# One hybrid attention block on one core: five forms of the last factor kept on chip, plain blocks written beside the second group, decays placed in the first pair

## The chip, the core and the metric

The kernel runs on one core of a Trainium2 chip. The engines of the core are TensorE (PE, matrix products), VectorE (DVE, elementwise work and scans), ScalarE (ACT, activations and casts), GpSimd (POOL) and SyncE (SP), which issues most of the transfers. Each engine executes its own instructions in order; between engines there are semaphores. The metric is the device time of one execution in microseconds, lower is better.

## The reference, cut to what matters

One layer on 512 tokens of width 2048, in fp32: a normalisation, one wide input projection, two groups of heads, gates, one output projection with the residual.

```python
h = rms_norm(x, norm_gain)
proj = einsum('bsd,de->bse', h, w_in)          # 14 groups of 512 columns and a rest of 16
(sb_q, sb_k, sb_v, sb_g, gl_q, gl_k, gl_v, gl_g, gl_lr) = split(proj)
a_out = stick_breaking_attention(rms_norm(q), rms_norm(k), v)     # 8 heads x 128
a_out = rms_norm(a_out) * silu(sb_g)
log_alpha = log_sigmoid(gl_lr @ gla_w_alpha + gla_b_alpha) / 16
b_out = gated_linear_attention(gl_q, gl_k, gl_v, log_alpha)       # 4 heads, key 128, value 256
b_out = rms_norm(b_out) * silu(gl_g)
x = x + concat([a_out, b_out]) @ w_out          # 4 groups of 512 columns
```

The cumulated log_alpha of a chunk gives the decay factors exp(cum) and exp(-cum), by which queries and keys of the second group are multiplied.

## The kernel before, in words

**Numbers.** A product in fp32 is made of three products of fp32r parts: every operand is split into hi (a cast, on ACT) and lo (the difference, on DVE). Weights are loaded from memory in tiles of 128 x 1024 (512 KB) by `load` (L162, tile names st_ and pw_) into three buffers st and four buffers pw, and `split` (L169 the cast, L170 the difference) fills one of three hi and three lo buffers.

**Groups.** The 14 + 4 groups of 512 weight columns go in this order: q and k (`direct`, eight steps each, one per weight tile), then eight pairs by `pair`: qv, vk, gqk, gv, ga, gb with the factor h, then o0 and o1 with the factor m. A pair is a product of 2 x 2 blocks with seven block products instead of eight. It has four parts: products A11 with D, then NQ with S4 (weight tiles b), then A12 with S3 (tiles c and d), then A22 (e, from pw). Tile names carry the pair and the part: hi_qvd2 is the hi part of tile d of unit 2 in pair qv. Units u are 0 to 3, in o0 and o1 in the order 0, 1, 3, 2. y and x are the two accumulators of a pair.

**Forms of the factor.** The factor of a pair is used in seven forms per unit: the plain blocks A11, A12, A22 and the sums D, NQ, S4, S3, each split into hi and lo (L279 to L283; 512 KB for both). The class `Acts` holds them. Forms named in its list `keep` stay on chip in slots of the ring u4 (25 slots of 512 KB, counted by `held`; `ut` takes one, `drop` gives some back, `room` asks). All other forms are put in one of four buffers of the pool as, written to memory once (`_write`, L255, far_ names) and read again by each later pair (L245). For h, `block` makes the plain blocks during q and writes them there; they stay in the ring until k is done. For both h and m the list is D and S3. The sums are made on DVE (L201 to L227).

**Work beside the products.** Attention, decays, gated linear attention and gates are generators ("side chains") that emit a few instructions each time a product calls `side.step()`. A chain that yields a number waits for that many microseconds of the planner's own clock `side.t`, which adds up a modelled duration of every matmul; one that yields a condition waits until that holds. The order of PE is the order in which the program emits its instructions. The orders of DVE, ACT, POOL and SP are made by a scheduler that prefers instructions emitted inside `urgent()`.

**Chains the change touches.** `decays` (L679 on) waits for the low-rank product, then 50 planner microseconds, then for five free slots; for each of four heads it makes one small matmul lg, on ACT lgs, three functions lge, the small amid and the factors qe, ke (L695 to L710), and on DVE L700, the scan L702, L707, gm L713, L715 and L716. It is spawned between the pairs qv and vk. `gate` (four of them, two halves each) multiplies a gate by its head outputs (ge, L980), waits 12 or 8 planner microseconds, transposes the result on PE (mT, L115) and fills the factor m (me, mo). `attention` makes scores zA, zB, zC, their cumulated sums cs_A, cs_B, cs_C (DVE L867 and L868), weights (ACT L873) and transposes them (wT_A, wT_B, wT_C).

`used` and `ready` are called by a pair at the start of its parts (0: A11, 2: NQ and S4, 3: A12 and S3) and give back slots; after q, k, qv, gb and o0 further slots are given back.

Of the kernel before, what the change touches and what calls it, by code (L numbers as in the profile page):

```python
# [15 lines left out]
D = 2048  # L16
# [77 lines left out]
def body(ctx: ExitStack, tc: tile.TileContext, x, xT, w_in, w_lr, w_alpha, vecs, w_out, out):  # L94
# [87 lines left out]
    class Acts:  # L182
# [74 lines left out]
        def block(self, odd, half, u, last):  # L257

            f = f"A{half + 1}{odd + 1}"
            if (f, u) not in self.near:  # L260
                name = f"{f}_{self.tag}{u}"
                with urgent():
                    if f == "A21":
                        t = wpool.tile([P, 2, KU, H2], F32R, name=name, tag="pw", bufs=HU)
                    else:
                        t = ut(name, F32R).rearrange("p h (k t) -> p h k t", k=KU)
                    self._split(t, f, u)
                    if f != "A21":
                        self._write(t, f, u, name)
                self.near[f, u] = t  # L270
            if last and f != "A21":
                drop(1)
            return self.near[f, u]
# [40 lines left out]
    def pair(A, s1, s2, tag, o1, o2, order=(0, 1, 2, 3), tmajor=True, before=None):  # L314
# [91 lines left out]
        o1.finish(y, 0, 1.0, m1)  # L406
        for u in order:
            w = split(pw[u], f"{tag}e{u}")
            mult("A22", u, w, x, False, u == last)
# [269 lines left out]
    def decays():  # L679
        yield lambda: "lr" in done  # L680
        yield 50.0
        yield room(5)
# [7 lines left out]
        for h in range(GH):  # L690
# [29 lines left out]
            if h < GH - 1:  # L720
                yield 8.0
        done.add("decays")
# [240 lines left out]
    def gate(gi):  # L963
# [3 lines left out]
        def chain(half, z):  # L967
# [13 lines left out]
            drop(1)  # L981
            yield 12.0 if gi < 2 else 8.0
            yield lambda: gi in me or held[0] + 2 <= NU4
# [33 lines left out]
    def used(stage, u):  # L1017
        if stage == 3 and u == 0:
            drop(6)

    direct(h, w_in[0], "q", normed("q0", qn[0]), before=first_loads)
    side.spawn(x_norm())
    direct(h, w_in[2], "k", normed("k0", kn[0]), extra=rank_products, last=True)
    side.spawn(low_rank())
    side.until(lambda: "rstd" in done)
    v[0] = ByToken("sv0", by_rstd)
    pair(h, w_in[1], w_in[4], "qv", normed("q1", qn[1]), v[0], before=used)
    drop(4)
    side.spawn(attention(0, qn[0], kn[0], v[0]))
    side.spawn(decays())  # L1030
    v[1] = ByToken("sv1", by_rstd)
# [9 lines left out]
    pair(h, w_in[6], w_in[7], "ga", gate(0), gate(1))  # L1041
    m = Acts("m", lambda u: me[u], lambda u: mo[u], ("D", "S3"))

# [4 lines left out]
    def ready(stage, u):  # L1048
        if stage == 0:
            side.until(lambda: m_done[u] == 2)  # L1050

    order = (0, 1, 3, 2)
    pair(m, w_out[0], w_out[1], "o0", Residual(0), Residual(1), order=order, before=ready)
    drop(10)
    pair(m, w_out[2], w_out[3], "o1", Residual(2), Residual(3), order=order)
# [44 lines left out]
```

## Time and profile before

| what | us |
|---|---|
| median of the runs | 901.11 (898.07 to 902.56, three runs) |
| the profiled execution | 900.33 |
| its span | 898.6 |
| PE busy | 823.4 (92%) |
| DVE busy | 627.7 (70%) |
| ACT busy | 517.3 (58%) |
| transfers | 216.99 MB, mean 241 GB/s |

The span runs from the first instruction to the last of the profiled execution; the granted clock of TensorE was 0.982 of full speed in the mean. q ends at about 61 us, k at 115, qv at 200, vk and gqk at 429, gv at 520, ga at 625, gb at 714, o0 at 814, o1 at 894. In a list of waits each row is an engine, what it waited to do, the releaser, the microseconds in total, how often, and the longest. A busy share is a mean over stages; what counts for a stage is which wait ends last in it.

### The profile page before, as it was taken

How to read it: one execution, taken by the hardware profiler on the slowest of the kernel's cores; microseconds unless marked ns; L12 is line 12 of the kernel's file. 1: busy time of each engine (PE TensorE's matmuls, PEld its weight loads, DVE VectorE, ACT ScalarE, POOL GpSimd, SP SyncE). 2: the span in 40 equal slices, each digit the busy share in tenths (PEclk: the TensorE clock that was granted, in tenths of full speed). 3: DMA queues.
4: the chain of work that ended last, by engine and by line, in shares of the span. 5: the costliest groups of instructions: out<-in, count | busy, mean ns of one | idle time of the engine just before them, and what ended most of it. 6: DMA issues, size and time to landing. Idle time of an engine off the chain costs nothing.

```text
span 898.6 us, 11580 instructions
## 1 busy us (share of the span) xinstructions
PE 823.4 (92%) x4082; PEld 684.2 (76%) x4082; DVE 627.7 (70%) x760; ACT 517.3 (58%) x947; POOL 68.5 (8%) x113
## 2 busy tenths in 40 slices
PE   7899989989998599989999899999998888889997
PEld 5688878778787499989787687877886766667875
DVE  4542858578777886788754685467956899786754
ACT  5465587358867598656563446556644745443322
POOL 1000000100132100210200010010001000000000
PEclk9999999999999799999999999999999999999999
DMA  8878327995497453787448971798579635999895
GB/s 311 299 288 297 138 81 246 295 367 193 164 282 213 143 207 125 253 225 263 162 163 266 335 270 64 247 290 307 197 252 303 236 140 207 313 347 394 283 328 164
DMA packets 62042, 216.99 MB, mean 241 GB/s; under 512 B 7040, under 2 KB 7168, under 8 KB 61984
## 3 DMA queue, kind: packets, MB, share of 16 engines
q1 hardware_dynamic: 54928, 195.26, 60.0%
q0 software_dynamic: 4608, 16.78, 10.3%
q10 hardware_dynamic: 2448, 4.21, 1.2%
q8 instruction: 32, 0.52, 0.2%
q14 instruction: 26, 0.21, 0.1%
HBM read 191.06 MB, written 25.17 MB: 241 GB/s over the span
## 4 chain that ended last, share of the span: by engine, by line
PE 21%; DMA 14%; DVE 9%; issue 3%; ACT 3%; DVEq 0%; SPq 0%; ACTq 0%
PE x_o L111 5%; PE y_o L111 4%; DMA st_gvd<-in_w_in 2%; PE y_gb L111 2%; PE x_gb L111 2%; PE x_ga L111 2%; DMA st_gad<-in_w_in 2%; DMA st_gbd<-in_w_in 2%; PE y_ga L111 1%; DMA st_o0d<-in_w_out 1%; DMA st_o1c<-in_w_out 1%; PE x_gv L111 1%; DMA pw_gb<-in_w_in 1%; DMA A_h<-far_A_h 1%; DMA A_m<-far_A_m 1%
## 5 line engine op out<-in xcount | busy, mean ns | idle before, releaser
L111 PE MATMUL z_q<-hi_q,A_h 128*128 128x512 f32 x128 | 33.3, 411 | 8.3 <-DVE A_h L283 3.3
L111 PEld LDWEIGHTS z_q<-hi_q,A_h 128*128 128x128 f32 x128 | 24.9, 197 | 16.4 <-DVE A_h L283 4.2
L111 PE MATMUL z_k<-hi_k,A_h 128*128 128x512 f32 x128 | 30.6, 391 | 0.0
L111 PEld LDWEIGHTS z_k<-hi_k,A_h 128*128 128x128 f32 x128 | 23.5, 188 | 4.8 <-ACT n_q L147 0.2
L170 DVE TENSOR_TENSOR lo_k<-st_k,hi_k 128x1024 fp32r<-128x1024 f32 x8 | 9.8, 1223 | 24.1 <-ACT hi_k L169 13.8
L180 POOL DMA_DIRECT2D pw_o<-in_w_out x8 | 7.0, 871 | 179.2 <-DVE S_m L283 79.5
L180 POOL DMA_DIRECT2D pw_qv<-in_w_in x4 | 3.6, 907 | 174.0 <-DVE st_qvd L175 174.0
L873 ACT ACTIVATE cs_B<-cs_B 128x512 f32<-128x512 f32 x8 | 5.1, 632 | 19.4 <-POOL cs_B L871 18.0
L111 PE MATMUL z_q<-lo_q,A_h 128*128 128x512 f32 x64 | 15.8, 389 | 0.0
L111 PE MATMUL z_k<-lo_k,A_h 128*128 128x512 f32 x64 | 15.8, 389 | 0.0
L115 PE MATMUL wT_B<-ident,cs_B 128*128 128x128 f32 x32 | 5.4, 294 | 11.0 <-DVE cs_A L868 10.4
L111 PE MATMUL x_o<-hi_o0d,S_m 128*128 128x512 f32 x32 | 10.0, 451 | 5.7 <-ACT hi_o0d L169 2.4
L115 PE MATMUL mT<-ident,ge 128*128 128x128 f32 x64 | 8.7, 280 | 6.0 <-DVE ge L980 6.0
L973 ACT ACTIVATE ge<-z 128x1024 f32<-128x1024 f32 x8 | 8.5, 1058 | 9.7 <-DVE z L969 9.7
L170 DVE TENSOR_TENSOR lo_q<-st_q,hi_q 128x1024 fp32r<-128x1024 f32 x8 | 9.7, 1225 | 6.2 <-ACT A_h L282 3.3
L111 PEld LDWEIGHTS z_q<-lo_q,A_h 128*128 128x128 f32 x64 | 12.0, 188 | 2.5
L111 PEld LDWEIGHTS z_k<-lo_k,A_h 128*128 128x128 f32 x64 | 12.0, 188 | 2.5
L175 DVE TENSOR_TENSOR st_gvd<-pw_gv,st_gvd 128x1024 f32<-128x1024 f32 x4 | 4.9, 1226 | 12.6 <-DMA st_gvd<-in_w_in 12.4
L595 ACT ACTIVATE xt<-xt 128x1024 f32<-128x1024 f32 x8 | 8.5, 1058 | 8.6 <-DMA xt<-in_x 8.5
L115 PEld LDWEIGHTS wT_B<-ident,cs_B 128*128 128x128 f32 x32 | 4.0, 150 | 12.3 <-DVE cs_A L868 10.8
L115 PEld LDWEIGHTS mT<-ident,ge 128*128 128x128 f32 x64 | 7.4, 142 | 7.8 <-issue 5.7
L111 PEld LDWEIGHTS x_o<-hi_o0d,S_m 128*128 128x128 f32 x32 | 6.4, 208 | 8.8 <-ACT hi_o0d L169 2.8
(630 smaller groups left out, 2645.8 us busy)
## 6 DMA issues: line engine op xcount, KB each, us to landing
A_h<-far_A_h SPq DMA_DIRECT2D x72, 512.0 KB, 6.1
NQ_h<-far_NQ_h SPq DMA_DIRECT2D x20, 512.0 KB, 4.3
S_h<-far_S_h SPq DMA_DIRECT2D x20, 512.0 KB, 4.2
far_A_h<-A_h SPq DMA_DIRECT2D x12, 512.0 KB, 4.5
far_A_m<-A_m SPq DMA_DIRECT2D x12, 512.0 KB, 7.3
A_m<-far_A_m SPq DMA_DIRECT2D x12, 512.0 KB, 8.0
st_q<-in_w_in SPq DMA_DIRECT2D x8, 512.0 KB, 5.4
st_k<-in_w_in SPq DMA_DIRECT2D x8, 512.0 KB, 4.9
```

The source lines that it names most:

```text
L111: nc.tensor.matmul(o, l, r, **kw)
L115: nc.tensor.transpose(o, i, ident)
L170: nc.vector.tensor_tensor(lo, t, hi.bitcast(F32), ALU.subtract)
L175: (eng or nc.vector).tensor_tensor(o, a, b, op)
L180: nc.gpsimd.dma_start(t, src, accum_op=ALU.add)
L595: nc.scalar.activation(xt, xt, AF.Square, accum_out=ss8[:, j * 2 + i:j * 2 + i + 1])
L873: nc.scalar.activation(cs, cs, AF.Exp)
L973: nc.scalar.activation(e, z, AF.Exp, scale=-1.0)
```

## The change

Four things are changed.

1. `block` no longer writes the plain blocks of h when they are made in q; the write is emitted at the block's last use, in k.
2. `decays` is spawned before pair qv and waits 4 planner microseconds instead of 50, and 10 instead of 8 between heads. Slots are given back accordingly: ten at part 3 of qv.
3. The wait of a gate before its transpositions is 12 planner microseconds for all but one half of gate 2, where it is 8; before it was 12 for gates 0 and 1 and 8 for gates 2 and 3.
4. For m the list `keep` becomes D, S4, S3, A12, A22: only A11 and NQ are written and read again. Slots for the three are found by giving back slots of me and mo during o0: `pair` calls `before` at part 4 too.

```diff
@@ block
                     self._split(t, f, u)
-                    if f != "A21":
-                        self._write(t, f, u, name)
                 self.near[f, u] = t
             if last and f != "A21":
+                with urgent():
+                    self._write(self.near[f, u], f, u, f"{f}_{self.tag}{u}")
                 drop(1)
@@ pair, last part
         for u in order:
+            if before is not None:
+                before(4, u)
             w = split(pw[u], f"{tag}e{u}")
@@ decays
         yield lambda: "lr" in done
-        yield 50.0
+        yield 4.0
...
             if h < GH - 1:
-                yield 8.0
+                yield 10.0
@@ gate
-            yield 12.0 if gi < 2 else 8.0
+            yield 8.0 if gi == 2 and half == 1 else 12.0
@@ the sequence of the program
         if stage == 3 and u == 0:
-            drop(6)
+            drop(10)
...
     side.spawn(low_rank())
+    side.spawn(decays())
...
     pair(h, w_in[1], w_in[4], "qv", normed("q1", qn[1]), v[0], before=used)
-    drop(4)
     side.spawn(attention(0, qn[0], kn[0], v[0]))
-    side.spawn(decays())
...
-    m = Acts("m", lambda u: me[u], lambda u: mo[u], ("D", "S3"))
+    m = Acts("m", lambda u: me[u], lambda u: mo[u], ("D", "S4", "S3", "A12", "A22"))
...
         if stage == 0:
             side.until(lambda: m_done[u] == 2)
+        elif stage == 3 and u == order[0]:
+            drop(2)
+        elif stage == 4 and u == order[0]:
+            drop(4)
...
-    drop(10)
+    drop(4)
     pair(m, w_out[2], w_out[3], "o1", Residual(2), Residual(3), order=order)
```

In the built program SP issues 24 transfers fewer; DVE, ACT and PE have the same instructions in another order. Three places show it. A row is the line, the operation, what it writes and from what, and the shape.

SP in the q stage, before (st_q are weight tiles, he and ho parts of the input, far_ the copies in memory of the plain blocks of h):

```order
L533 DMA ho0_154<-in_xT 128x1024
L255 DMA far_A11_h0_125<-A11_h0_122 128x1024
L162 DMA st_q01_202<-in_w_in 128x1024
L162 DMA st_q11_262<-in_w_in 128x1024
L255 DMA far_A12_h0_167<-A12_h0_164 128x1024
L255 DMA far_A22_h0_172<-A22_h0_169 128x1024
L533 DMA he1_198<-in_xT 128x1024
L162 DMA st_q02_306<-in_w_in 128x1024
L162 DMA st_q12_348<-in_w_in 128x1024
L533 DMA ho1_240<-in_xT 128x1024
```

and now:

```order
L535 DMA ho0_152<-in_xT 128x1024
L162 DMA st_q01_196<-in_w_in 128x1024
L162 DMA st_q11_254<-in_w_in 128x1024
L162 DMA st_q02_294<-in_w_in 128x1024
L535 DMA he1_192<-in_xT 128x1024
L162 DMA st_q12_334<-in_w_in 128x1024
L162 DMA st_q03_374<-in_w_in 128x1024
L535 DMA ho1_232<-in_xT 128x1024
L255 DMA far_A11_h0_500<-A11_h0_122 128x1024
L162 DMA st_q13_414<-in_w_in 128x1024
L255 DMA far_A22_h0_555<-A22_h0_165 128x1024
L255 DMA far_A12_h0_553<-A12_h0_162 128x1024
L255 DMA far_A11_h1_637<-A11_h1_202 128x1024
```

The writes of A11, A12, A22 of unit 0 and A11 of unit 1 have moved behind ho1; the rows of SP that follow stand nearly as they did, with the other writes among them.

DVE at the end of pair vk, before (lgs, lge, gm, qe, ke belong to the decays; vke and gqka to the products; e_A and cs_A to the attention):

```order
L700 SCALAR_TENSOR_TENSOR lgs1_2500<-lgs1_2500,lge1_2502 128x512
L861 SCALAR_TENSOR_TENSOR e_A011_2611<-zA011_2606,e_A011_2611 128x512
L170 TENSOR_TENSOR lo_vke3_2764<-pw_vk3_1848,hi_vke3_2763 128x1024
L175 TENSOR_TENSOR pw_gqk2_2953<-pw_gqk2_2953,st_gqka2_2951 128x1024
L702 SCALAR_TENSOR_TENSOR lge1_2502<-blk_2408,lgs1_2500 128x512
L867 SCALAR_TENSOR_TENSOR cs_A011_2617<-runs_86,e_A011_2611 128x512
L707 TENSOR_TENSOR lgs1_2500<-lge1_2502 128x512
L868 TENSOR_TENSOR cs_A011_2617<-zA011_2606,cs_A011_2617 128x512
L713 TENSOR_TENSOR gm1_2513<-qe0_2411,amid1_2508 128x3
L715 SCALAR_TENSOR_TENSOR qe0_2411<-qe0_2411,rbc_105 128x512
L716 TENSOR_TENSOR ke0_2412<-ke0_2412,rbc_105 128x512
```

DVE in the second half of pair qv, now:

```order
L702 SCALAR_TENSOR_TENSOR lgs0_1415<-lgs0_1415,lge0_1417 128x512
L175 TENSOR_TENSOR st_qvd2_1490<-pw_qv2_1068,st_qvd2_1490 128x1024
L170 TENSOR_TENSOR lo_qvc2_1493<-st_qvc2_1488,hi_qvc2_1492 128x1024
L704 SCALAR_TENSOR_TENSOR lge0_1417<-blk_1406,lgs0_1415 128x512
L170 TENSOR_TENSOR lo_qvd2_1498<-st_qvd2_1490,hi_qvd2_1497 128x1024
L709 TENSOR_TENSOR lgs0_1415<-lge0_1417 128x512
L170 TENSOR_TENSOR lo_qvc3_1552<-st_qvc3_1547,hi_qvc3_1551 128x1024
L715 TENSOR_TENSOR gm0_1428<-qe0_1409,amid0_1423 128x3
L718 TENSOR_TENSOR ke0_1410<-ke0_1410,rbc_105 128x512
L175 TENSOR_TENSOR st_qvd3_1549<-pw_qv3_1107,st_qvd3_1549 128x1024
L717 SCALAR_TENSOR_TENSOR qe0_1409<-qe0_1409,rbc_105 128x512
L170 TENSOR_TENSOR lo_qvd3_1557<-st_qvd3_1549,hi_qvd3_1556 128x1024
```

The pieces of the decays, which stood among the last tiles of vk and ahead of cs_A, now stand among the tiles c and d of qv.

SP in pair o0, in the part with A12 and S3, before (A_m names are plain blocks of m, xr parts of the residual input):

```order
L162 DMA st_o0c1_6867<-in_w_out 128x1024
L255 DMA far_S4_m2_6776<-S4_m2_6770 128x1024
L255 DMA far_NQ_m2_6801<-NQ_m2_6798 128x1024
L255 DMA far_A12_m0_6836<-A12_m0_6833 128x1024
L162 DMA st_o0d1_6869<-in_w_out 128x1024
L162 DMA st_o0c3_6915<-in_w_out 128x1024
L255 DMA far_A12_m1_6884<-A12_m1_6881 128x1024
L162 DMA st_o0d3_6917<-in_w_out 128x1024
L255 DMA far_A12_m3_6932<-A12_m3_6929 128x1024
L162 DMA st_o0c2_6963<-in_w_out 128x1024
L162 DMA st_o0d2_6965<-in_w_out 128x1024
```

and now:

```order
L245 DMA A11_m0_7099<-far_A11_m0_6374 128x1024
L162 DMA st_o0c1_6857<-in_w_out 128x1024
L255 DMA far_NQ_m2_6793<-NQ_m2_6790 128x1024
L162 DMA st_o0d1_6859<-in_w_out 128x1024
L245 DMA A11_m1_7122<-far_A11_m1_6414 128x1024
L162 DMA st_o0c3_6903<-in_w_out 128x1024
L245 DMA A11_m3_7161<-far_A11_m3_6483 128x1024
L245 DMA A11_m2_7200<-far_A11_m2_6543 128x1024
L162 DMA st_o0d3_6905<-in_w_out 128x1024
L162 DMA st_o0c2_6949<-in_w_out 128x1024
L162 DMA st_o0d2_6951<-in_w_out 128x1024
```

The writes of S4, A12 and A22 are gone; reads of A11, which stood behind them for pair o1, have moved up between the loads c and d.

## Rows read from the trace of the kernel before

**Rows 1.** Windows: start:end, length, busy PE, PEld, DVE, ACT, POOL; clock, DMA share, GB/s.
```profile
200.00:270.00 70.00, 67.61 (x342) 55.87 (x340) 53.59 (x62) 55.92 (x123) 11.54 (x23) 1.00 0.65 218
714.00:771.00 57.00, 48.94 (x208) 36.59 (x207) 56.67 (x72) 32.62 (x45) 0.86 (x1) 1.00 0.56 189
771.00:794.00 23.00, 17.47 (x73) 13.02 (x71) 16.40 (x20) 9.79 (x14) 2.09 (x3) 1.00 1.00 309
794.00:814.00 20.00, 18.38 (x73) 14.81 (x74) 17.56 (x21) 8.04 (x9) 0.53 (x1) 0.91 1.04 379
814.00:894.00 80.00, 76.50 (x334) 62.34 (x334) 49.29 (x48) 26.12 (x25) 3.48 (x4) 1.00 0.88 296
```

**Rows 2.** Waits of PE over the span: us in total, times, longest.
```profile
PE wT_B L115 <- DVE cs_A L868: 10.4, 1, 10.4
PE mT L115 <- DVE ge L980: 6.0, 3, 3.6
PE x_qv L111 <- ACT hi_qvd L169: 4.0, 2, 3.1
PE x_o L111 <- ACT hi_o1d L169: 3.3, 2, 2.0
...
PE x_o L111 <- ACT hi_o0d L169: 2.4, 1, 2.4
...
PE x_o L111 <- DMA A_m<-far_A_m: 1.4, 1, 1.4
```

**Rows 3.** Timeline of PE: start, us, instructions, idle before and its releaser.
```profile
20.56 0.51 PE L111 MATMUL z_q<-hi_q,A_h 128*128 128x512 f32 x1 [1.59 <-ACT A_h L282]
...
38.45 0.49 PE L111 MATMUL z_q<-hi_q,A_h 128*128 128x512 f32 x1 [1.35 <-ACT A_h L282]
...
293.79 1.07 PE L111 MATMUL x_vk<-lo_vke,A_h 128*128 128x512 f32 x4
305.26 1.12 PE L115 MATMUL wT_B<-ident,cs_B 128*128 128x128 f32 x4 [10.40 <-DVE cs_A L868]
...
688.44 1.40 PE L115 MATMUL mT<-ident,ge 128*128 128x128 f32 x8 [3.62 <-DVE ge L980]
```

**Rows 4.** Groups of DVE from 286.9 to 305.25: busy us, mean ns, idle before.
```profile
L702 DVE TENSOR_TENSOR_SCAN lge<-blk,lgs 128x512 f32<-128x512 f32 x2 | 2.4, 1222 | 0.0
...
L700 DVE SCALAR_TENSOR_TENSOR lgs<-lgs,lge 128x512 f32<-128x512 f32 x2 | 1.4, 682 | 0.0
L707 DVE TENSOR_TENSOR lgs<-lge 128x512 f32<-128x512 f32 x2 | 1.4, 680 | 0.0
...
L716 DVE TENSOR_TENSOR ke<-ke,rbc 128x512 f32<-128x512 f32 x1 | 0.7, 683 | 0.0
L715 DVE SCALAR_TENSOR_TENSOR qe<-qe,rbc 128x512 f32<-128x512 f32 x1 | 0.7, 682 | 0.0
```

**Rows 5.** Timeline of ACT, three places.
```profile
302.94 0.21 ACT L705 ACTIVATE amid<-lge 128x4 f32<-128x4 f32 x1 [7.38 <-DVE lge L702]
...
687.25 1.04 ACT L169 CAST hi_gbd<-st_gbd 128x1024 fp32r<-128x1024 f32 x1 [4.87 <-DVE st_gbd L175]
...
774.40 0.62 ACT L282 CAST A_m<-mo 128x512 fp32r<-128x512 f32 x1 [2.63 <-DMA far_NQ_m<-NQ_m]
```

**Rows 6.** Windows of 10 us, columns as in the first group.
```profile
170.00:180.00 10.00, 8.45 (x36) 6.68 (x36) 6.07 (x6) 3.85 (x4) 1.74 (x2) 1.00 0.93 272
220.00:230.00 10.00, 10.00 (x48) 8.38 (x47) 6.78 (x7) 10.00 (x25) 0.54 (x2) 1.00 0.32 105
300.00:310.00 10.00, 4.74 (x13) 3.90 (x14) 8.16 (x12) 6.28 (x24) 1.46 (x4) 0.50 0.26 92
```

**Rows 7.** Transfers from 770 to 814: queue, count, KB each, us to landing.
```profile
DMA packets 4744, 14.94 MB, mean 340 GB/s; under 512 B 525, under 2 KB 525, under 8 KB 4742
...
far_A_m<-A_m SPq DMA_DIRECT2D x7, 512.0 KB, 7.9
...
st_o0d<-in_w_out SPq DMA_DIRECT2D x2, 512.0 KB, 8.9
```

## The prediction

> **What bounds the kernel now.** I read the windows by stage first [rows 1]: TensorE (PE) is the bound almost everywhere, and what can be won is its idle time and its slow clock. In 714 to 771 us it is different: VectorE (DVE) is busy 56.67 of 57.00 us while PE works 48.94, so the first half of pair o0 ends when DVE has done its work. Then the waits of PE over the whole span [rows 2], longest sum first. One wait stands out, 10.4 us for cs_A, a tile of the attention. Next come mT (6.0 in three), hi_qvd (4.0), hi_o1d (3.3), hi_o0d (2.4) and 1.4 for a reload of A_m. Last I read the timelines and groups at the places of the change: PE [rows 3], DVE in the long gap [rows 4], ACT [rows 5], windows of 10 us [rows 6] and the transfers at the end of o0 [rows 7].
>
> The long gap: PE starts the last matmuls it can at 293.79 and the next instruction, a transposition wT_B that waits for the attention's sum cs_A, at 305.26 [rows 3]. DVE works practically without a pause from 287 to 305.25: its decay groups show no idle time before them [rows 4]. ScalarE (ACT), which runs in order, stands 7.38 us in front of amid, the small exponential of a decay, until DVE has scanned lge [rows 5]. So DVE's queue sets the end of that gap, and decays are part of the queue. The granted clock from 300 to 310 is 0.50, that is 1.2 GHz, behind a stretch in which PE stood idle [rows 6].
>
> **The change part by part.** The sum is made against the profiled execution, 900.33 us, which lies 0.8 under the median of 901.11.
>
> (1) Plain blocks of h. In the code the twelve writes of A11, A12, A22 leave the q stage for the k stage. In the built order only those of u = 0 and the first of u = 1 move; the others stand at SyncE (SP) where they stood. Before step 3 of q, he1 stood behind three of these writes, each of which waits for DVE. Now one weight load more, st_q02, stands ahead of it and no write. The idle 1.59 us that end at 20.56 [rows 3] should go. Against it: st_k00 and the reads of A11_h0 and A11_h1 stand ahead of he2, and the second read must now wait for a write that was issued later. he2 feeds the matmul at 38.45, which waited 1.35 us [rows 3]; if it lands no earlier than now, this gap grows by the same 1.6 us. I take **0**, from -2 (only the first gap changes) to +2 (he2 lands later by about as much again). The k stage keeps its SP order, and none of PE's waits of [rows 2] lies there.
>
> (2) Decays. Each of the four heads costs DVE six instructions, by the means of [rows 4] 0.68 + 1.22 + 0.68 + 0.68 + 0.68 and a small one, about 4 us. ACT has seven for it, of the same tile but for one; I estimate them at the same 4. The work is the same in all; 16 us on each engine leave the last part of pair vk and the start of gqk for the second half of qv and the first of vk. Three parts follow.
> - In the gap's own DVE queue, 287.0 to 305.25, decays take 2.4 + 1.4 + 1.4 + 0.7 + 0.7 = 6.6 us [rows 4]. DVE had no idle there, so cs_A comes 6.6 us earlier.
> - What is left of the gap is 10.4 - 6.6 = 3.8 us. Decay work before 287 is gone too, which pulls the attention forward as far as DVE was the limit; DVE was busy 53.59 of 70 us in 200 to 270 [rows 1], so not all of it counts. I take 2 of the 3.8.
> - The clock: the 4.7 us from 305.26 to 310 at half speed cost 2.4; with a short gap I count 1.5 of it back.
>
> That is -10.1. Against it stands the new place. In the second half of qv, PE waits 4.0 us for hi_qvd, which waits for the subtraction st_qvd on DVE [rows 2]. In the built order ke of head 0 (0.7) and a smaller piece stand ahead of st_qvd3, and similar ones ahead of others: I take +1.1, from 0 to +4 (some 1 us for every head). DVE has room there, ACT too (6.07 and 3.85 of 10 us at 170 to 180); later ACT is full for stretches (10.00 of 10.00 at 220 to 230) [rows 6], and two heads fall there. Sum **-9.0**, range -14 (10.4 + 2.4 + 1, no gap left and nothing lost) to +2 (the gain of 6.6 spent on new waits, and a clock that falls elsewhere).
>
> (3) Gates. Three pieces of mT move one or two products later. The largest wait for mT is 3.6 of the 6.0 us. There PE would next need hi_gbd2, whose cast ACT starts at 687.25 [rows 5], only 1.2 us before the transposition starts at 688.44 [rows 3]. So about 1 us goes: **-1**, from -2 to +1.
>
> (4) Pair o0, first half: the same DVE instructions, DVE full: **0**. Its S4, A12 and A22 are computed as before and no longer written.
>
> (5) Pair o0 from 771 to 814: PE works 17.47 of 23 and 18.38 of 20 us, and the clock of 0.91 in the second stretch costs 0.09 x 20 = 1.8; lost in all 5.5 + 1.6 + 1.8 = 8.9 us [rows 1]. DVE and ACT have time there; the DMA engines have none (1.00 and 1.04 busy). 14.94 MB pass from 770 to 814, and the d loads take 8.9 us to land [rows 7]. PE waits there for hi_o0d and A_m [rows 2]; hi_o0d hangs on a load, and ACT stands 2.63 us ahead of 774.40 in front of A_m until a write has emptied a slot [rows 5]. Seven of those writes go [rows 7], 3.7 MB or 25%. The A11 reads stay in this stretch, in the built order between the loads c and d. The nearest row for what then remains is pair o1, at 296 GB/s and a DMA share of 0.88: PE loses 80.00 - 76.50 = 3.5 in all [rows 1]. 8.9 - 3.5 = 5.4 is my lower value; all 8.9 the upper one. As the ACT waits go too, I take **-6**, range -1 (A11 reads take the place of the writes) to -9. It contains the 1.4 us wait at o1's start: A11 is then already read.
>
> By the Trainium skill, page "DMA: Bandwidth & Descriptors", section "Specifications", a core gets about 358 GB/s from memory. By that figure the 14.94 MB would need an estimated 41.7 of these 44 us and the bytes themselves would be the bound; with 11.3 MB an estimated 31.5 us, no bound at all. The page would give the upper value, 9. The trace doesn't agree with it as a limit: 379 GB/s passed from 794 to 814 [rows 1].
>
> (6) Pair o1: twelve of its twenty reads go. PE lost 3.5 us there, 3.3 of it before hi_o1d [rows 1, 2]. Pairs that read from memory at a smaller rate still lose some (200 to 270 us: 2.4 at 218 GB/s), so I take **-2.5**, from 0 to -3.5.
>
> Sum: 0 - 9.0 - 1 + 0 - 6 - 2.5 = -18.5; 900.33 - 18.5 = **881.8**, say 882.
>
> **Rivals.**
> - *The gap moves.* The attention is a chain over DVE, ACT and PE; if latency, not DVE's queue, sets cs_A, the gap reappears some steps later and decays bring only 1 us. For it: ACT stood idle beside a busy DVE. Against it: DVE has 0.0 idle at each of those decay groups [rows 4]. Time: 900.3 - 1 - 1 - 6 - 2.5 = 890.
> - *Reads take the place of writes* in o0: -1.4 there and -1 in o1. For it: the DMA share stays near 1.00 when SP fills the time with prefetch. Time: 900.3 - 9 - 1 - 1.4 - 1 = 888.
> - *Bytes alone were the bound* of 771 to 814, the mechanism by which all of its loss goes: -8.9, and -3.5 in o1. Time: 900.3 - 9 - 1 - 8.9 - 3.5 = 878. It is the case that the figure of the skill's page above favours.
> - *Slower: decays block ACT in the first pairs.* ACT runs in order; amid waits for the scan on DVE as it did for 7.38 us [rows 5]. In qv and vk the casts hi_qvd, hi_qve, hi_vka stand behind it, and PE stands behind those. Full price, four heads: 4 x 7.4 = 29.6; without the gain of (2): 900.3 - 9.5 + 29.6 = 920. It decides from about 1.3 such waits on (9.5 / 7.4); two give 906. Against it: in the new place DVE is not full, so the scan comes within its own 1.2 us.
>
> A further doubt is that (1) does not do what it says: by the built order it mostly doesn't, which is in the sum.
>
> **How the numbers follow.** Forecast 882, own range 873 to 888: 0.58. Gap moves, 890: 0.15. Reads take the place, 888: 0.12. Bytes alone, 878: 0.08. Slower, 906 and up: 0.07. The first two rivals together (896) are part of the second and third chance. A measurement of this kernel tells 0.5%, some 4.5 us, from no change, so the border lies at 896.6. Faster 0.87, same 0.06, slower 0.07. The range goes from 869, all lower ends of the steps together (900.3 - 2 - 14 - 2 - 9 - 3.5 = 869.8), to 897, the two joined rivals; what is left out below and above is some 0.1.
>
> **What would show it.** Step (2): wT_B no longer among PE's waits at over 4 us, the clock near 300 us at 1.00, and hi_qvd's 4.0 grown by 1 to 2. Step (1): no gap before step 3 of q, a longer one before step 5. Step (5): no ACT wait for a far write in o0, landings of st_o0d near 6 us, PE's loss after the first half of o0 near 3. Step (6): SP's waits for PE in o1 gone. The prediction is wrong if a new wait over 5 us stands between 160 and 250 us, if cs_A still ends a gap of that size, or if the first half of o0 changes by more than 2 us.

## The result, and the profile after

The changed kernel takes 889.53 us in the median of four runs, beside 900.08 for the kernel before; the ratio is 0.988 (0.984 to 0.991). In a second group, on another chip, it is 0.9925 (0.9896 to 0.9954). It is faster, by 10.6 us in the first group and by 6.1 in the second (897.13 to 891.00), where 18.5 were forecast. The median lies in the whole range of 869 to 897, which the rivals had widened, but outside the 873 to 888 that the forecast claimed for its own mechanism; it stands where two rivals were put, at 888 and 890. So the time alone confirms little, and the account has to go by stages. The profiled execution takes 887.69, 12.6 less than that of before.

Where the time went shows in a table by stage. A stage is counted from the first matmul of its first product to that of the next stage, in one trace each; the second pair of columns is from the second chip. o1 is counted to its last matmul. "o0, c to e" are the parts with A12, S3 and A22.

| stage, us | before | after | before, 2nd | after, 2nd | forecast difference |
|---|---|---|---|---|---|
| q | 53.1 | 58.0 | 52.3 | 55.6 | 0 |
| k | 54.5 | 53.4 | 54.1 | 55.2 | 0 |
| qv | 85.1 | 85.3 | 83.0 | 87.0 | +1.1 |
| vk and gqk | 228.8 | 219.2 | 228.3 | 219.2 | -10.1 |
| gv, ga | 195.8 | 194.3 | 194.9 | 196.5 | 0 |
| gb | 88.5 | 86.0 | 88.6 | 87.0 | -1 |
| o0, first half | 57.3 | 59.5 | 57.4 | 61.8 | 0 |
| o0, c to e | 43.0 | 40.6 | 40.8 | 41.1 | -6 |
| o1 | 80.5 | 77.7 | 80.3 | 78.1 | -2.5 |

Two traces of one kernel differ by up to 2.4 us in a stage here. The second pair shows places and not the gain: its trace of the changed kernel is the longest of ten runs, its trace of the kernel before (893.3) lies below that chip's median, and its differences add up to a loss of 1.8 us. What stands in both pairs is: vk with gqk gained 9 to 10, o1 2 to 3, gb 2; q lost 3 to 5, the first half of o0 2 to 4; the end of o0 won 2 in one pair and nothing in the other.

The page of the profile after (the first line is the span, then busy time by engine, and the queues):

```profile
span 886.0 us, 11528 instructions
...
PE 821.5 (93%) x4082; PEld 686.5 (77%) x4082; DVE 627.2 (71%) x760; ACT 516.1 (58%) x947; POOL 70.8 (8%) x113
...
DMA packets 58586, 204.40 MB, mean 231 GB/s; under 512 B 6656, under 2 KB 6784, under 8 KB 58528
```

12.6 MB fewer are moved, 24 transfers of 512 KB, as the built order said. The waits of PE over the span (engine, what waits, releaser, us in total, times, longest) answer to [rows 2]:

```profile
PE x_qv L111 <- ACT hi_qvd L169: 5.1, 1, 5.1
PE z_q L111 <- ACT A_h L282: 4.8, 1, 4.8
PE x_o L111 <- DVE S_m L283: 4.7, 1, 4.7
PE y_o L111 <- ACT D_m L282: 3.2, 1, 3.2
```

The 10.4 us for cs_A at wT_B are gone, and so are hi_o1d and the reload of A_m. Three waits of about 5 us stand now: in q and in o0, where there was none of that length, and in qv, where it was 3.1. Windows of the places (length, busy PE, PEld, DVE, ACT, POOL; clock, DMA share, GB/s) answer to [rows 1, 6]:

```profile
180.00:190.00 10.00, 4.86 (x14) 3.55 (x13) 6.05 (x7) 4.03 (x7) 0.88 (x1) 0.66 1.02 320
290.00:300.00 10.00, 10.00 (x60) 8.78 (x59) 7.93 (x10) 6.18 (x21) 1.07 (x4) 1.00 0.68 243
765.00:775.00 10.00, 5.05 (x15) 3.51 (x14) 5.74 (x8) 2.19 (x3) 0.86 (x1) 0.76 1.02 333
```

The stretch around 300, which had a clock of 0.50, is full now. But 180 to 190 and 765 to 775 each have a long stop and a low clock. In the window 804 to 882 (o1) PE works 76.88 of 78.00 us:

```profile
763.50:804.00 40.50, 35.55 (x146) 28.66 (x145) 31.77 (x39) 18.04 (x24) 2.62 (x3) 0.92 0.99 313
804.00:882.00 78.00, 76.88 (x337) 62.70 (x335) 52.16 (x52) 26.43 (x26) 3.48 (x4) 1.00 0.61 185
```

### The profile page after: what moved, and what is told of

Read it like the earlier page. It is cut to its first block, busy times and chain, and to the rows that moved or that the text cites. A ratio compares the mean times of both kernels' runs of the same rounds, so it can differ in the third digit from the quotient of the medians.

```text
span 886.0 us, 11528 instructions
## 1 busy us (share of the span) xinstructions
PE 821.5 (93%) x4082; PEld 686.5 (77%) x4082; DVE 627.2 (71%) x760; ACT 516.1 (58%) x947; POOL 70.8 (8%) x113
## 3 DMA queue, kind: packets, MB, share of 16 engines
q0 software_dynamic: 4608, 16.78, 10.7%
## 4 chain that ended last, share of the span: by engine, by line
PE 27%; DMA 10%; DVE 9%; ACT 2%; issue 2%; DVEq 0%; ACTq 0%
PE x_o L111 7%; PE y_o L111 4%; PE x_ga L111 3%; PE x_gb L111 3%; PE y_ga L111 2%; PE y_gb L111 2%; DMA st_gbd<-in_w_in 2%; PE x_gv L111 2%; PE y_gv L111 2%; PE o L111 1%; DMA st_o1d<-in_w_out 1%; DMA st_gad<-in_w_in 1%; DMA st_gvc<-in_w_in 1%; DMA pw_o<-in_w_out 1%; DMA st_o0d<-in_w_out 1%
## 5 line engine op out<-in xcount | busy, mean ns | idle before, releaser
L111 PE MATMUL z_q<-hi_q,A_h 128*128 128x512 f32 x128 | 36.9, 446 | 9.7 <-ACT A_h L282 4.8
L111 PEld LDWEIGHTS z_q<-hi_q,A_h 128*128 128x128 f32 x128 | 27.7, 219 | 18.3 <-ACT A_h L282 5.5
L170 DVE TENSOR_TENSOR lo_k<-st_k,hi_k 128x1024 fp32r<-128x1024 f32 x8 | 9.8, 1223 | 24.5 <-PE lr_ps L111 10.4
L111 PE MATMUL x_qv<-hi_qvd,S_h 128*128 128x512 f32 x32 | 9.7, 454 | 5.1 <-ACT hi_qvd L169 5.1
L149 ACT ACTIVATE on<-a,r_a 128x128 f32<-128x128 f32 x32 | 9.1, 366 | 9.1 <-DVE r_a L570 9.1
L975 ACT ACTIVATE ge<-z 128x1024 f32<-128x1024 f32 x8 | 8.5, 1058 | 10.2 <-DVE z L971 10.2
L111 PE MATMUL y_o<-hi_o0p,D_m 128*128 128x512 f32 x32 | 9.8, 450 | 4.4 <-ACT D_m L282 3.2
L869 DVE TENSOR_TENSOR_SCAN cs_B<-runs,e_B 128x512 f32<-128x512 f32 x8 | 9.8, 1224 | 3.8 <-POOL e_B L866 3.8
L111 PEld LDWEIGHTS x_qv<-hi_qvd,S_h 128*128 128x128 f32 x32 | 7.0, 222 | 7.1 <-ACT hi_qvd L169 5.6
```

Of the source, the lines that this page charges most:

```text
L111: nc.tensor.matmul(o, l, r, **kw)
L149: nc.scalar.activation(dst, src, AF.Copy, scale=scale)
L170: nc.vector.tensor_tensor(lo, t, hi.bitcast(F32), ALU.subtract)
L869: nc.vector.tensor_tensor_scan(cs[:, ::-1], rst[:, ::-1], sp[:, ::-1], 0.0, ALU.mult, ALU.add)
L975: nc.scalar.activation(e, z, AF.Exp, scale=-1.0)
```

## The new stop in q, followed back

PE reaches step 5 at 36 us and waits for the block made of he2 until 41.17; then its first sixteen matmuls take 6.56 us, where the same step took 3.70 for fifteen before. The timeline of PE:

```profile
34.34 1.99 PE L111 MATMUL z_q<-lo_q,A_h 128*128 128x512 f32 x8
41.17 6.56 PE L111 MATMUL z_q<-hi_q,A_h 128*128 128x512 f32 x16 [4.84 <-ACT A_h L282]
```

The timeline of SP shows why he2 came late (start, us that the issues span, count):

```profile
27.36 0.33 SPq L162 DMA_DIRECT2D st_k<-in_w_in  x1
27.79 4.07 SPq L245 DMA_DIRECT2D A_h<-far_A_h  x2
31.91 0.43 SPq L628 DMA_DIRECT2D lr_st<-in_w_lr  x1
...
33.31 1.15 SPq L535 DMA_DIRECT2D he<-in_xT  x1
```

Two reads of A11 span 4.07 us instead of 0.43 for one: by the built order the second waits for the landing of the write of the same block, and that write was issued within the group at 22.29, where it had stood at 21.26. By the trace the write landed at 31.52 and the second read was issued at 31.54; in each of the four other traces with all writes late the two also lie 0.02 us apart. he2 is issued at 33.31; before it was 30.45. The gap ahead of step 3 [rows 3] did go, as forecast. (In this trace the first sixteen matmuls of q took 5.56 us, not 3.94, which alone would have hidden that gap; but it is absent too in two traces of late writes where they took 3.92 and 3.93.)

**Writes put back.** All twelve writes return to where the blocks are made.

```diff
                     self._split(t, f, u)
+                    if f != "A21":
+                        self._write(t, f, u, name)
...
-                with urgent():
-                    self._write(self.near[f, u], f, u, f"{f}_{self.tag}{u}")
                 drop(1)
```

> The changed kernel with only the writes of h put back where the blocks are made. In the changed kernel q runs from 7.74 to 65.50 us, before from 7.78 to 60.61; PE waits 4.8 us for the block made of he2, which was issued 2.9 us later than before because SP stands 4.07 us at the two reads of A11, the second of which waits for its own late write. Theory (late write holds SP): q is again 53 us long, ends near 60.6, and the time falls by 4 to 5 us to about 885; the gap ahead of step 3 (2 us) is back. Rival (q's loss is a slow clock at the start, 1.6 us in its first step, and chance): q ends at 63 or later and the time stays within 2 us of the changed kernel.

q is 53.0 us, and the wait ahead of step 5 is short again (timeline of PE and of SP):

```profile
38.21 0.50 PE L111 MATMUL z_q<-hi_q,A_h 128*128 128x512 f32 x1 [0.69 <-ACT A_h L282]
```

```profile
29.84 0.42 SPq L535 DMA_DIRECT2D he<-in_xT  x1
```

The theory holds for the stage: 5.0 us less than in the changed kernel. The gap ahead of step 3 did not come back, as PE came to it 1.5 us later after a slow first step. q is short although its first step ran at a low clock here too (5.54 us for sixteen matmuls, in the changed kernel 5.56), so the rival is out. The size is less sure than these two traces make it: q takes 54.0 to 58.0 us in the five traces with all writes late, and 52.3 to 54.5 in the eight with all of them early; the means are 2.4 us apart. The median is 886.98, ratio 0.9895 (0.985 to 0.994); the runs spread from 879.69 to 891.01, and the whole time doesn't tell it from the changed kernel. The stage does.

**One write put back.** Only that of A11 of unit 1.

```diff
                     self._split(t, f, u)
+                    if (f, u) == ("A11", 1):
+                        self._write(t, f, u, name)
...
             if last and f != "A21":
-                with urgent():
-                    self._write(self.near[f, u], f, u, f"{f}_{self.tag}{u}")
+                if (f, u) not in self.far:
+                    with urgent():
+                        self._write(self.near[f, u], f, u, f"{f}_{self.tag}{u}")
```

> The changed kernel with one write alone, that of A11 of unit 1, put back where the block is made; the other eleven stay late. Theory (SP is held at the read of A11_h1 by that block's own late write): SP issues he2 near 29.5 instead of 33.3, the 4.8 us wait before step 5 falls to 1 us or less, the gap ahead of step 3 stays away, and q is 7 us shorter than in the changed kernel; time about 882. Rival (the number of transfers ahead of he2 decides, not that one wait): he2 is issued at 32 or later and less than 2 us are gained.

The timeline of SP:

```profile
28.67 0.80 SPq L245 DMA_DIRECT2D A_h<-far_A_h  x2
...
31.01 0.86 SPq L538 DMA_DIRECT2D he<-in_xT  x1
```

Both readings miss. SP's 4.07 us at the reads become 0.80, and he2 is issued at 31.01, 2.3 us earlier; but the wait at step 5 falls from 4.8 to 3.5, not below 1, and q from 58.0 to 55.7, which is also what the changed kernel takes on the second chip (55.6). So this run does not show what share of the loss is the read's wait for its own write. It shows what ended the wait next (timeline of ACT):

```profile
36.54 0.50 ACT L638 CAST lr<-lr_st 128x128 fp32r<-128x128 f32 x2 [9.96 <-DMA lr_st<-in_w_lr]
...
38.26 0.72 ACT L534 ACTIVATE he<-he,vec 128x512 f32<-128x512 f32 x1
```

ACT stands in front of the small load lr_st until 36.54 and comes to he2 only then, with no wait for he2's own load. lr_st was issued at 29.51, 2.4 us earlier than in the changed kernel, and by the trace it landed at 36.46, 0.2 earlier; in the kernel before it landed at 34.0. Both reads of A11 and the three late writes were issued ahead of it. That these transfers made it slow is argued from the order; no run separated it. Median 886.42, ratio 0.991 (0.988 to 0.994).

## The decays, alone and undone

**Decays back.** The changed kernel with the chain spawned after qv, waits of 50 and 8 planner microseconds, and slots given back as before.

```diff
-    side.spawn(decays())
     side.until(lambda: "rstd" in done)
...
+    drop(4)
     side.spawn(attention(0, qn[0], kn[0], v[0]))
+    side.spawn(decays())
...
-        yield 4.0
+        yield 50.0
         yield room(5)
...
-                yield 10.0
+                yield 8.0
```

> The changed kernel with the decays back in pair vk (spawned after qv, waits 50 and 8, slots given back as before); nothing else. Theory (the decays on DVE ahead of cs_A made the 10.8 us gap): the gap at wT_B is back, vk and gqk take 228 us instead of 219, qv loses less before hi_qvd, and the time rises by 8 to 10 us to about 899. Rival (the gap was moved by the earlier stages, not by the decays): vk and gqk stay within 3 us of 219.

The old wait is back in full, and the one in qv is short again (PE's waits over the span; the second from the window 160 to 200):

```profile
PE wT_B L115 <- DVE cs_A L870: 10.3, 1, 10.3
```

```profile
PE x_qv L111 <- ACT hi_qvd L169: 2.0, 1, 2.0
```

vk and gqk take 229.8, 10.6 more than in the changed kernel; qv takes 82.8, 2.5 less. Median 892.58, ratio 0.997 (0.995 to 1.000). The theory holds for the stages; by the ratios the whole rises by 4 to 9 us.

**Decays only**: the kernel before with the reverse of that diff.

> The kernel before with the decays in the first pair alone. Theory: vk with gqk 9 to 10 us shorter (219), qv 2 to 3 us longer before hi_qvd, all else as before; time 6 to 8 us less, 0.991 to 0.993. Rival (the gain needs the other parts): less than 3 us.

Median 890.79 beside 898.34, ratio 0.991 (0.987 to 0.994): 7.6 us, where the whole change brings 10.6 and 6.1. vk and gqk 219.4, qv 87.2, with 6.3 us before hi_qvd.

So the decays explain the gain, and qv pays 2 to 4 us for it. How it pays was not as forecast. DVE after, in qv:

```profile
175.04 1.22 DVE L704 TENSOR_TENSOR_SCAN lge<-blk,lgs 128x512 f32<-128x512 f32 x1
176.17 1.20 DVE L170 TENSOR_TENSOR lo_qvd<-st_qvd,hi_qvd 128x1024 fp32r<-128x1024 f32 x1
...
179.80 0.69 DVE L718 TENSOR_TENSOR ke<-ke,rbc 128x512 f32<-128x512 f32 x1
183.65 1.23 DVE L175 TENSOR_TENSOR st_qvd<-pw_qv,st_qvd 128x1024 f32<-128x1024 f32 x1 [3.17 <-DMA st_qvd<-in_w_in]
```

At 183.65 DVE does not come from a decay but from 3.17 us of waiting for the load of st_qvd3. The timeline of SP there, before and after:

```profile
173.23 0.33 SPq L162 DMA_DIRECT2D st_qvd<-in_w_in  x1
173.65 0.94 SPq L245 DMA_DIRECT2D A_h<-far_A_h  x2
...
172.66 0.85 SPq L245 DMA_DIRECT2D A_h<-far_A_h  x1
175.15 0.33 SPq L162 DMA_DIRECT2D st_qvd<-in_w_in  x1
```

Counted from the first product with a tile c (161.5 before, 163.9 after) the load is issued no later, at 11.2 us where it was 11.7. But a read of A_h now stands ahead of it, and it takes 8.5 us to land where it took 5.6. In all nine traces with the decays early it takes 8.0 to 10.2 us, in the five others 5.4 to 6.1. The buffer of a load is freed by a lo subtraction, and the decay pieces had pushed those back; that this put the read first is argued, not shown. So the pieces cost twice: their own time, and a load that lands later.

**Decays behind the tiles d.** To see whether that price can be avoided, decays and kept forms alone (writes and gates as before) with 20 planner microseconds more ahead of the decays.

```diff
         yield room(5)
+        yield 20.0
         wa, lrT = low[0][:, 0, :], low[0][:, 1, :]
```

> The kernel with the decays in the first pair and the kept forms (writes and gates as before), with the decays 20 planner microseconds later, so that on DVE and ACT they begin behind the tiles c, d and e of qv, at the start of vk. Theory (pieces of decays ahead of st_qvd3 lengthen the wait for hi_qvd from 3.1 to 6.5 us): that wait is 3 to 3.5 us again, qv 83 us instead of 87, vk with gqk 219 to 222, time 2 to 4 us below that kernel, about 0.982 to 0.984 of the kernel before. Rival (qv's loss comes from elsewhere, or vk cannot take the decays): the wait for hi_qvd stays over 5 us, or vk with gqk grows by 4 us or more; no gain.

Its waits of PE over the span:

```profile
PE T_q L115 <- DVE cs_B L871: 3.4, 1, 3.4
PE wT_A L115 <- ACT cs_A L876: 3.2, 2, 3.0
...
PE x_gv L111 <- DVE gv L443: 2.9, 1, 2.9
...
PE x_qv L111 <- ACT hi_qvd L169: 2.4, 1, 2.4
```

qv is 81.8 us and its wait 2.4: the theory on the cause holds. But vk with gqk is 222.9, 2.4 longer than in the kernel named next, and gv 94.4, 4.7 longer, where PE now waits 2.9 us for gv; the attention's last matmul stands 50 us into gv, 31 in the kernel named next, and that the one makes the other is not shown. Median 890.27, ratio 0.990 (0.988 to 0.993): no gain, the second rival. Part of the gv difference may be the chip, since the two were not run side by side.

## Pair o0: where the forecast gain stayed

The chain of the stop at d0 of o0, on DVE after:

```profile
764.92 0.69 DVE L208 TENSOR_TENSOR s_m<-me 128x512 f32<-128x512 f32 x1
769.87 1.23 DVE L175 TENSOR_TENSOR st_o0d<-pw_o,st_o0d 128x1024 f32<-128x1024 f32 x1 [4.26 <-DMA st_o0d<-in_w_out]
771.01 0.69 DVE L283 TENSOR_TENSOR S_m<-s_m,S_m 128x512 fp32r<-128x512 f32 x1
```

PE starts the product with S3_m0 at 766.57, does one matmul, and stops until S3's difference part is there (the last row). It takes 0.69 us and could have run at about 766.5, when ACT had made the cast, but stands in DVE's queue behind the subtraction on st_o0d1, whose load had not landed. The product takes 10.05 us instead of 2.72. The rest of the two parts runs at 2.7 to 3.2 us each, where before four of them took 4.0 to 6.5 and the last one 4.3. What was won there is lost in one place. The load behind that stop is not faster: st_o0d1 took 8.9 us to land where it took 9.6 before, and 9.3 beside 8.2 on the second chip. Only the two d loads after it landed sooner, in 6.9 and 4.2 us where it was 10.2 and 7.6. PE's waits for hi_o0d and A_m are gone.

**S3 first.** In the changed kernel, S3 of the first unit is made ahead of the part's weight loads.

```diff
         elif stage == 3 and u == order[0]:
             drop(2)
+            m.get("S3", u)
```

> The changed kernel with the form S3 of unit 0 of m made ahead of the part with A12 and S3 of pair o0; nothing else. In the changed kernel DVE stands 4.26 us in front of the subtraction on st_o0d1, whose load is under way, and the difference part of S3_m0 lies behind it, so that PE stops 5.19 us in the product x_o of d0 and 7.3 us are lost in it. Theory (the order on DVE is the cause): that product is 2.7 to 3.5 us long, a stall of at most 2 us remains at d1, and the time falls by 4 to 7 us to about 884. Rival (the loads are the cause, and the order only shows where): the stall moves to d1 or c1 and the time falls by less than 2 us.

The stop at d0 is gone (3.2 us), but the product ahead of it takes 6.2, since the difference part of A12_m0 has now gone behind two lo subtractions and two further pieces; c to e is 38.8, 1.2 to 2.3 less than in the kernels that ran as the changed one there. o1 is 80.8, longer by 3, with short waits for lo in its first half (1.4 us in three). Median 887.82, ratio 0.992 (0.989 to 0.995). The stop moved by one product, so neither reading is settled by this run.

**Kept forms only.** The kernel before with `keep` of m, the slots given back and `before(4, u)`, as in the diff of the change, and nothing else.

> The kernel before with one part of the change: S4, A12 and A22 of m stay on chip, slots given back as the change does; writes of h, decays and gates as before. Theory (what the kept forms give in o0 is taken back by the new order on DVE, in which the difference part of S3_m0 stands behind a load, and o1 alone gains): the stages up to gb are those of the kernel before, o0 within 1 us of it with one stall of 4 us or more at S3_m0, o1 2 to 3 us shorter; time 2 to 4 us less. Rival (the gate waits, not the kept forms, made o0 as long as it was): o0 is 4 us shorter or more, and the time 6 us or more less.

The waits of DVE from 745 to 800:

```profile
DVE st_o0d L175 <- DMA st_o0d<-in_w_out: 5.4, 2, 2.8
```

The theory falls here. c to e takes 37.1 us (on this chip 40.8 before, 41.1 after); o0 95.1 instead of 98.2. There is no stop at S3_m0: in this kernel its difference part stands ahead of st_o0d1, as the timeline of DVE shows:

```profile
768.10 1.22 DVE L170 TENSOR_TENSOR lo_o0d<-st_o0d,hi_o0d 128x1024 fp32r<-128x1024 f32 x1
769.24 0.69 DVE L283 TENSOR_TENSOR S_m<-s_m,S_m 128x512 fp32r<-128x512 f32 x1
769.84 1.28 DVE L511 TENSOR_TENSOR o0y<-o0y,x_o 128x512 f32<-128x512 f32 x2
773.96 1.22 DVE L175 TENSOR_TENSOR st_o0d<-pw_o,st_o0d 128x1024 f32<-128x1024 f32 x1 [2.84 <-DMA st_o0d<-in_w_out]
```

The kept forms alone give 3.7 us there, not 6, and the order that took them back is not theirs. o1 gained nothing in this trace (80.5; one stop of 2.3 us in its second product, while its last parts fell from 36.7 to 34.6). Median 893.48 beside 897.13, ratio 0.996 (0.993 to 0.999).

**Gates back.** The changed kernel with the gate waits of before.

```diff
-            yield 8.0 if gi == 2 and half == 1 else 12.0
+            yield 12.0 if gi < 2 else 8.0
```

> The changed kernel with the waits of the gates as before (12 for gates 0 and 1, 8 for 2 and 3); nothing else. In its built order the difference part of S3_m0 stands on DVE ahead of the subtraction on st_o0d1 again, as in the kernel that only keeps the forms (37.1 us for the last two parts of o0), where the changed kernel has it behind (40.6). Theory (the gate waits cost in o0 what they win in gb, both by three transpositions that moved into o0 and by the order on DVE that followed): gb is 2 to 3 us longer (88 to 89), the first part of o0 2 us shorter (57.5), its last two parts 3 to 4 us shorter with no stall over 3 us; time 2 to 4 us below the changed kernel, 0.985 to 0.988 of the kernel before. Rival (what follows in o0 is due to the decays or to chance): the stall at S3_m0 stays and the time is that of the changed kernel or above.

The waits of PE from 765 to 810:

```profile
PE y_o L111 <- DVE A_m L283: 3.3, 1, 3.3
```

That is the only one there. d0 takes 2.7, c to e 37.9; a stop is left, at a later tile c, whose product takes 7.9 us, so "no stall over 3 us" was missed. gb is 88.8, as expected 2.8 longer. The first half of o0 is 59.5, not 57.5, in this trace, with products as in the kernel before but for one of 5.5. Median 888.14, ratio 0.988 (0.984 to 0.992): the stages moved as the theory said, the whole time is that of the changed kernel. So the gate waits win 2 to 3 us in gb and lose them in o0. That the order on DVE at d0 hangs on them is shown, as nothing else differs; how the scheduler came to it is not. The expectation's three moved transpositions are one: by the traces three of the eight pieces of mT start after o0's first matmul in the changed kernel, and two did before.

**Order by hand.** Writes back, and for every unit of o0 A12 and S3 made ahead of the unit's loads.

```diff
-        elif stage == 3 and u == order[0]:
-            drop(2)
+        elif stage == 3:
+            if u == order[0]:
+                drop(2)
+            m.get("A12", u)
+            m.get("S3", u)
```

> The changed kernel with the writes of h put back where the blocks are made, and in pair o0 the forms A12 and S3 of a unit made ahead of that unit's weight loads, so that on DVE their difference parts stand ahead of the subtraction on the next unit's load. Theory (two orders, one on SP and one on DVE, cost what the prediction expected): q 53, o0 95 us with no stall of 4 us in the part with A12 and S3, time 8 to 10 us below the changed kernel, about 0.978 of the kernel before. Rival (the loads bound that part of o0): o0 98 or more, the stall stands at a later product, and only the 4 to 5 us of q are gained.

A miss. q is 52.4, but c to e is 43.3, longer than in any other kernel: the stops stand at the third product (6.4) and at d2 (7.2). The waits of PE from 740 to 805, and one of DVE from 745 to 800:

```profile
PE y_o L111 <- DVE lo_o0c L170: 2.5, 1, 2.5
PE x_o L111 <- DVE S_m L283: 1.8, 1, 1.8
```

```profile
DVE st_o0d L175 <- DMA st_o0d<-in_w_out: 5.1, 2, 3.6
```

DVE waits 5.1 us for loads in this part, as it does in the kernel with the kept forms alone (5.4) and in the changed kernel (4.3 in the one wait shown). The rival is right so far: in all eleven traces with the kept forms DVE waits 4.8 to 6.2 us for the d loads of c to e, in the three without them 1.5 to 4.8; the order decides what stands behind them. Median 887.76, ratio 0.992 (0.989 to 0.995).

**Decays and kept forms.** The two parts of the change that gain, without writes and gates.

> Two parts of the change alone, the decays in the first pair and the five kept forms; the writes of h and the gates as before. Theory (writes and gates cost more than they give): q 53, vk with gqk 219, gb 88.5, o0 95, o1 79 us; time 4 to 8 us below the changed kernel, 0.980 to 0.985 of the kernel before. Rival (the parts depend on each other): one of these stages is 3 us longer than named and the time that of the changed kernel.

The longest wait of PE over the span:

```profile
PE x_qv L111 <- ACT hi_qvd L169: 6.5, 1, 6.5
```

q 52.8, vk with gqk 220.5, gb 89.3, o0 95.7 with c to e 37.6, o1 79.3: each within 1.5 us of what was named, but qv is 87.4 with its 6.5 us. Median 886.54 beside 898.34, ratio 0.986 (0.983 to 0.989), the lowest of all, just outside the 0.980 to 0.985 expected. It does not stand clear of the changed kernel, whose intervals are 0.984 to 0.991 and 0.990 to 0.995; by the stages of the traces it is 3 to 5 us better in q and 3 to 3.5 in the end of o0, and 2 to 3 worse in gb.

**The changed kernel and the kernel before once more**, for the stages on one chip:

> The changed kernel itself once more, beside the other kernels of this group, so that stages are compared on one chip. It should stand to the kernel before as 0.988, and q should be about 57 us, the pair vk with gqk 219, pair o0 100, pair o1 78.

> The kernel before once more, for its stages on the same chip as the others: q 53, vk with gqk 229, gb 88, o0 100, o1 80 us.

The stages are those of the table. The changed kernel's trace was the longest of its ten runs (895.22, clock 0.968; the shortest 883.43), and o0 was 103 in it, not 100. d0 of o0 took 10.7 us again, and q lost 3.3.

## Why the prediction was right and wrong, by its steps

The traces of all kernels, sorted by the part of the change that touches a stage, give each step a size (us, lowest to highest, number of traces, from several chips; a run that edits the stage in a way of its own is left out). gv with ga, which no part touches, lies between 191.9 and 196.5 in them, so a difference of 1 or 2 us is weak unless the two ranges stand apart.

| stage and part | as before | as changed | difference of means |
|---|---|---|---|
| q, writes | 52.3 to 54.5 (8) | 54.0 to 58.0 (5) | +2.4 |
| qv, decays | 82.8 to 85.1 (4) | 85.3 to 89.4 (9) | +3.2 |
| vk and gqk, decays | 228.3 to 231.0 (4) | 217.4 to 220.5 (9) | -10.3 |
| gb, gates | 88.5 to 89.3 (7) | 85.6 to 87.4 (7) | -2.5 |
| o0, first half, gates | 57.3 to 59.6 (7) | 59.4 to 61.8 (7) | +1.6 |
| o0, c to e, kept forms, gates as before | 39.4 to 43.0 (3) | 37.1 to 37.9 (4) | -3.5 |
| o0, c to e, kept forms and gates | 39.4 to 43.0 (3) | 40.0 to 41.1 (5) | -0.4 |
| o1, kept forms | 80.3 to 80.5 (3) | 77.4 to 80.8 (11) | -1.7 |

The rows of the whole change (all but the sixth) add up to -7.7, between the 10.6 and the 6.1 us of the two groups.

- **(2) Decays, -9: right.** vk and gqk fell by 9.6 and 9.1 where -10.1 were reckoned, cs_A's wait is gone, the clock at 300 is 1.00; qv took back 0.2 and 4.0 where 1.1 was reckoned, within its bounds. The gap closed wholly, so the 6.6 us by the sum of DVE's pieces was too careful, and the price in qv was too small: what was counted was the piece ahead of one subtraction, not the load that lands later. The rival that the gap moves is refuted by the run with the decays back.
- **(1) Writes of h, 0: wrong,** +3.3 and +4.9. The step named the right instructions: the first gap did go, he2 did come late, for the reason given. It priced the second as an equal trade. It named the read of A11_h1 that waits for its own write, but gave that wait no length (SP stood 4.07 us at the two reads, 3.2 to 3.5 in the other four traces), and it left out that a stop of 4.8 us is followed by a step at a low clock (6.56 us instead of about 4). The upper bound of +2 was set equal to the lower one, with no row behind it.
- **(3) Gates, -1, and (4) first half of o0, 0: sign wrong together.** gb gained 2.5 and 1.6, the first half of o0 lost 2.2 and 4.4. That half is bound by DVE [rows 1], and one transposition more, with what it releases, stands in it; the step costed only the place that it left. With the gates put back that half was still 59.5 in the one trace, so its loss rests on the table's row, where the two ranges overlap.
- **(5) o0, c to e, -6: wrong,** -2.4 and +0.3. The gain is there and somewhat over-sized: kept forms with the gates of before give -3.5, as PE's waits for hi_o0d and A_m go; but DVE waits for the d loads as long as before or longer, and the load at the stop lands no faster. Its failed step is "as the ACT waits go too, I take -6": a stop was left out that stood in the built order, S3_m0 behind st_o0d1 on DVE. That order came with the gate waits, an edit that the prediction costed at its own place only.
- **(6) o1, -2.5: right,** -2.8 and -2.2, though with the kept forms alone nothing was gained in the one trace.

Two of the signs that the prediction named for being wrong did come: a wait over 5 us between 160 and 250 us (5.1 for hi_qvd, 5.7 on the second chip), and a first half of o0 changed by more than 2 us. Of its other signs, the ACT wait for a far write in o0 is gone, but PE's loss after that half is 5.0 us (40.50 - 35.55), not 3.

The rival "reads take the place of writes" gave 888, near what came, and its sign is there: the DMA share stayed at 0.99, and from 760 to 804 13.58 MB passed, 1.4 fewer than in those 44 us before, where the step took off 3.7. But it does not set the time: with the kept forms and the gates of before the share is 0.96 to 0.99 as well, and c to e takes 37.1 to 37.9. "Bytes alone" is out: those 13.58 MB passed at 309 GB/s where it had been 340 [rows 7], and the stretch is hardly shorter; with d0 at 2.72 it would be. The figure of the Trainium skill (page "DMA: Bandwidth & Descriptors", section "Specifications") that favoured it did not bound this stretch. "Decays block ACT" is out as priced: the wait in qv is 4.6 to 7.2 us in nine traces, one in each, not four of 7.4, and it is DVE that waits, for a load.

What stays open: how q's loss divides between the read that holds SP and the late writes ahead of lr_st and he2; why o1 gains nothing with the kept forms alone; and whether an order exists in which o0's last parts lose less than the 4.5 us (37.1 - 32.6, twelve products of 2.72) that remain with the kept forms alone.

## What to carry to other kernels

Cost an edit of the planner's waits also at the place to which the work moves, and read there, on each in-order engine, what the built order puts behind an instruction that waits for a load: a difference of 0.7 us behind a load cost 7 here. When a store is moved later, look for the read of the same data in the same queue, and at what stands behind that read. Work moved from an engine's queue into a part with few load buffers costs its own time and then the loads that land later for it. And when the issue of a load is compared between two traces, count both from the start of the same part, or a stage that began 4 us later looks like a late load.

## What the runs showed of the hardware

Not expected in its size was the price of the clock. Behind each stop of about 5 us the matmuls ran at a lower clock: 6.56 us for sixteen in q instead of 3.79, 3.78 for eight in qv instead of 1.98, and in o0 a product with 4.7 us of stop that was longer by 7.3. The granted clock was 0.66 from 180 to 190 and 0.76 from 765 to 775. So a stop of 5 us cost 7 to 8. Shorter stops went both ways. Ahead of step 5 of q a stop of 1.35 us before was followed by fifteen matmuls in 3.70, one of 1.81 (decays behind the tiles d) by fifteen in 5.29; at the end of o0 before, one of 2.37 was followed by eight in 3.26 instead of 1.98. So what a stop costs was not to be read off its length alone.

The changed kernel's ten single runs on one chip differ by 12 us, with mean clocks from 0.968 to 0.980. The longest has the lowest clock, but runs of 883.43 and 893.11 have 0.978 and 0.977, so the mean clock does not explain that spread.
